# Splitting ten weight blocks of a hybrid encoder layer in two pieces each instead of one

## The chip, the core and the metric

The kernel runs on one core of a Trainium2 chip. The metric is the device time of one execution in microseconds (us). The engines are called as the profile calls them: PE (matrix multiply), PEld (its weight loads), DVE (vector), ACT (scalar and activation), POOL, and SP, which issues nearly all DMAs. Each engine works through its own list of instructions in a fixed order that was settled when the program was built; an instruction that waits holds up everything behind it on its engine.

## The reference, cut to what matters

One layer serves 512 prompt tokens and 64 sample tokens with the same weights:

```
proj = rmsnorm(x) @ w_in              # 1024 -> conv inputs, z, a, b, qd, kd, vd
oa = gated_delta_rule(conv(...)) ; oa = rmsnorm(oa) * silu(z)
ob = rmsnorm(differential_attention(qd, kd, vd))   # 4 heads of 128 columns
h = x + concat(oa, ob) @ w_out
h = h + memory_attention(rmsnorm(h)) ; h = h + square(relu(rmsnorm(h) @ W1)) @ W2
```

The gated delta rule works in chunks: for each chunk a unit triangular 128x128 system per head is inverted, and a state is carried from chunk to chunk.

## The kernel before

Weights come in blocks of 128 columns: a tile `raw` of [128, 8, 128], that is eight row blocks of 128 rows. All arithmetic is float32 made of two rounded parts, so each block is split by `split_weights` into a high part `wh` (a cast on ACT, L161) and a low part `wl = raw - wh` (a subtraction on DVE, L162). `project` then runs two column ranges of the tokens (256, then 320), and in each the eight row blocks in turn, every one with the products high x high, high x low and low x high, into one PSUM bank of the tag `pr`, of which there are three. There are three buffers for `raw` and two each for `wh` and `wl`, so the split of a block can begin when the block two before it has gone through PE.

The middle of the program holds these pieces:

- `project_z` (L635): four blocks, whose result goes through Silu. In the lists they are `pr_246` to `pr_262`.
- `gdn_prep` (L649) prepares a chunk of the delta rule: transposes, score products, then levels 2, 4, 8, 16, 32 of a blockwise inversion. A level is two transposes into the bank of a chunk's tag and `Dt,B` products, a copy X on ACT (L762), a masked copy Y on DVE (L763), products `Y,X` on PE, and two subtractions on DVE (L770, L771) with which the next level begins. Even chunks use bank `g0`, odd chunks `g1`. After the levels come a transpose of Dt, `Dt,At` products, a copy on ACT (L779), `X,Y` products and a negated copy on DVE (L783).
- `gdn_scan` (L811) carries the state: `on,X` products in bank `gs`, DVE (L830), products with the state and KQ, `vn,kd`, then a norm over ACT (L801), DVE (L802), POOL and DVE (L809), and a transpose of `on`.
- `diff_project` (L961) projects q, k and v of an attention head, one block each; `diff_head` does the attention itself.

The source has `prep` of chunk 0, then for each chunk the prep of the next one, `project_z` (once) and the scan; then the four heads. A list scheduler with estimated costs turns that into the engines' orders. It pulls the blocks of `project_z` and of the first two heads forward between the dependent steps of the delta rule, where they serve PE as filler. Instructions under `tc.high_priority()`, as the splits are, go ahead of others that are ready.

Of the kernel before, what the change touches and what calls it, by code (L numbers as in the profile page):

```python
# [8 lines left out]
F32 = mybir.dt.float32  # L9
F32R = mybir.dt.float32r  # L10
AF = mybir.ActivationFunctionType
ALU = mybir.AluOpType
# [3 lines left out]
P = 128  # L16
D = 1024
KT = 8
# [19 lines left out]
def hybrid_layer_kernel(  # L38
# [10 lines left out]
    V, A, G = nc.vector, nc.scalar, nc.gpsimd  # L49
# [29 lines left out]
    def nm(s):  # L79
        uid[0] += 1  # L80
        return f"{s}_{uid[0]}"

    def pair(slot, dt=F32):

        return up.tile([P, 2, 4, T], dt, tag=f"u{slot}", name=nm("u"))
# [6 lines left out]
    def small(tag, shape, bufs=None, dt=F32):  # L92
        tag = SHARED.get(tag, tag)
        bufs = 1 if tag in ("vn", "on", "S", "qz") or tag[:-1] in ("At", "Dt", "Y") else 2
        return sp.tile(shape, dt, tag=tag, name=nm(tag), bufs=bufs)
# [4 lines left out]
    def bank(tag="ba"):  # L100
        return ps.tile([P, 512], F32, tag=tag, name=nm(tag), bufs=BANKS[tag])
# [4 lines left out]
    def mm(out, lhsT, rhs, start=True, stop=True, pin=False, skip_group_check=False):  # L106
        i = nc.tensor.matmul(out, lhsT, rhs, start=start, stop=stop, skip_group_check=skip_group_check)  # L107
        if pin:
            tc.keep_in_program_order(i)

    def tr(out, in_, pin=False):
        n = in_.shape[0]
        i = nc.tensor.transpose(out, in_, ident[:n, :n])  # L113
        if pin:
            tc.keep_in_program_order(i)
# [36 lines left out]
        nc.sync.dma_start(raw, w[:, c0 : c0 + P].rearrange("(k p) n -> p k n", p=P))  # L152
        return raw

    def split_weights(w, shape):
        raw = wp.tile(shape, F32, tag="raw", name=nm("raw"), bufs=3)
        nc.sync.dma_start(raw, w.rearrange("(k p) n -> p k n", p=P))
        wh = wp.tile(shape, F32R, tag="wh", name=nm("wh"))
        wl = wp.tile(shape, F32R, tag="wl", name=nm("wl"))
        with tc.high_priority():  # L160
            A.copy(wh, raw)  # L161
            V.tensor_tensor(wl, raw, wh.bitcast(F32), ALU.subtract)  # L162
        return wh, wl

    def weights(w, c0, kt=KT):

        return split_weights(w[:, c0 : c0 + P], [P, kt, P])

    def project(w, x, evac, kt=KT, halves=HALVES, between=None):


        for a0, n in halves:
            b = bank("pr")
            for k in range(kt):
                low_part = lambda: mm(b[:, :n], w[1][:, k, :], x[k // 4][:, 0, k % 4, a0 : a0 + n], start=False, stop=False)
                if k == kt - 1:
                    low_part()
                high_parts(b, w[0], x, k, a0, n, kt)
                if k < kt - 1:
                    low_part()  # L180
            if between and a0 == 0:
                between()
            evac(b[:, :n], a0, n, None if a0 else b[:, 256:])

    def high_parts(b, w, x, k, a0, n, kt=KT):
        xk = x[k // 4][:, :, k % 4, a0 : a0 + n]
        if a0 == 0:
            mm(b.rearrange("p (j n) -> p j n", j=2), w[:, k, :], xk, start=k == 0, stop=k == kt - 1)
        else:
            mm(b[:, :n], w[:, k, :], xk[:, 0], start=k == 0, stop=False)  # L190
            mm(b[:, :n], w[:, k, :], xk[:, 1], start=False, stop=k == kt - 1)

    def add_to(dst, b, more):
        A.copy(dst, more)
        V.tensor_tensor(dst, b, dst, ALU.add)
# [50 lines left out]
    xs = [pair(i, F32R) for i in (0, 1)]  # L246
    w2 = w_in[0]
# [387 lines left out]
    def project_z():  # L635
        for h in range(H):
            def evac(b, a0, n, more):
                z = zs[:, h, a0 : a0 + 256]
                with tc.high_priority():
                    if more is not None:  # L640
                        add_to(z, b, more)
                        b = z
                    A.activation(z, b[:, :256], AF.Silu)
                    if a0:
                        A.activation(zsample[:, h, :], b[:, 256:], AF.Silu)

            project(weights(w2, 1536 + h * P), xs, evac)

    def gdn_prep(c, nb, L):  # L649
        (ck, kb), (cq, qb), (_, vblk) = (blocks(typ, c, L) for typ in (1, 0, 2))  # L650
# [310 lines left out]
    def diff_project(h):  # L961
        hs = slice(h * P, (h + 1) * P)
        if h < 2:
            qn = [od[:, 2 * h + j, :SEQ].bitcast(F32R) for j in range(2)]
        else:
            qn = [small(tag, [P, SEQ], dt=F32R) for tag in ("Y0", "Y1")]
        tags = ("kd", "vb", "X", "KQ") if h % 2 else ("At0", "At1", "Dt0", "Dt1")
        ks = [small(tag, [P, SEQ], dt=F32R) for tag in tags]
        stacked[h] = ks[:2], ks[2:]
        for kind, base in (("q", 2056), ("k", 2568), ("v", 3080)):  # L970
            def evac(b, a0, n, more):
                ts_ = slice(a0, a0 + n)
                t0 = slice(a0, min(a0 + n, SEQ))
                n0 = t0.stop - a0

                def parts(dst, src):
                    A.copy(dst[0][:, t0], src[:, :n0])
                    V.tensor_tensor(dst[1][:, t0], src[:, :n0], dst[0][:, t0].bitcast(F32), ALU.subtract)

                if kind == "q":  # L980
                    d = b
                    if more is not None:
                        d = qn[1][:, ts_].bitcast(F32)
                    with tc.high_priority():
                        if more is not None:
                            add_to(d, b, more)
                        parts(qn, d)
                    if a0:
                        for c in range(2):
                            R = slice(64 * c, 64 * c + 64)  # L990
                            A.copy(qz[R, R], d[R, n - DEC :])
                            for j in range(2):
                                nc.sync.dma_start(
                                    qs[h % 2][64 * j : 64 * j + 64, c, :SEQ].bitcast(F32), qn[j][R].bitcast(F32)
                                )
                    return
                d = small("zr", [P, 320])[:, :n] if kind == "v" else kdT[:, h, ts_]
                with tc.high_priority():
                    if more is not None:
                        add_to(d, b, more)  # L1000
                    else:
                        V.tensor_copy(d, b)
                if kind == "k":
                    parts(stacked[h][0], d)
                    if a0:
                        first_, second_ = ([x.bitcast(F32) for x in pair_] for pair_ in stacked[h])
                        for j in range(2):
                            for R in (slice(0, 64), slice(64, P)):
                                nc.sync.dma_start(second_[j][R], first_[j][64:])
                        for j in range(2):  # L1010
                            nc.sync.dma_start(first_[j][64:], first_[j][:64])
                bt = bank()
                for t in range(2):
                    tr(bt[:, t * P : (t + 1) * P], d[:, t * P : (t + 1) * P])
                if a0:
                    tr(bt[:DEC, 256:384], d[:, 256:])
                src, t2 = bt[:, :256].rearrange("p (t d) -> p t d", t=2), slice(a0 // P, a0 // P + 2)
                if kind == "v":
                    A.copy(vtm[:, t2, hs], src)
                    if a0:  # L1020
                        A.copy(vs[:DEC, h, :], bt[:DEC, 256:384])
                else:
                    ko = small("ko", [P, 3, P])
                    A.copy(ko[:, :2], src)
                    nc.sync.dma_start(o_dk_p[0, 0, a0 : a0 + 256, h, :].rearrange("(t p) d -> p t d", p=P), ko[:, :2])
                    if a0:
                        A.copy(ko[:DEC, 2], bt[:DEC, 256:384])
                        nc.sync.dma_start(o_dk_s[0, 0, :, h, :], ko[:DEC, 2])

            project(weights(w2, base + h * P), xs, evac)  # L1030
        nc.sync.dma_start(o_dv_p[0, 0, :, h, :].rearrange("(t p) d -> p t d", p=P), vtm[:, :, hs])
        nc.sync.dma_start(o_dv_s[0, 0, :, h, :], vs[:DEC, h, :])

# [100 lines left out]
    for h in range(H):  # L1134
        diff_project(h)
        next(sample, None)
        if h == 0:
            diff_cache()
        finish = diff_head(h, finish)
        next(sample, None)  # L1140
# [237 lines left out]
    raws, parts = {}, {}  # L1378
# [334 lines left out]
```

## Time and profile before

| | |
|---|---|
| time, median of 3 runs | 979.46 us (977.47 to 980.0) |
| the profiled execution's own time | 979.61 us |
| its span, first to last instruction | 976.5 us |
| granted PE clock, mean | 0.997 |
| PE, DVE, ACT busy | 98%, 71%, 55% |
| the splits of the ten blocks | from about 97 to 199 us of the span |

The profiled time is 3.1 us longer than its span, for what lies around the program, and 0.15 us above the median. A view of groups lists, for a line, engine and pair of tiles, the count, the busy time, the mean duration of one and the idle time of the engine just before. A timeline row gives start, duration, engine, line, operation, tiles and count, and in brackets the engine's idle time before it with what ended it. PE's matmuls overlap, so its durations exceed the distance from one start to the next.

### The profile page before, as it was taken

To read this page: it belongs to the slowest core of one execution; us is meant where nothing else is said; L and a number is where in the kernel's file an instruction comes from. 1 tells how busy PE (TensorE), PEld (TensorE's weight loads), DVE (VectorE), ACT (ScalarE), POOL (GpSimd) and SP (SyncE) were. 2 spreads that over 40 slices of the span, in tenths; PEclk is the share of its full clock that TensorE was granted. 3 is DMA by queue.
4 is the path that set the end of the run, shared out by engine and by line. 5 is a ranking of instruction groups with operands and counts; after the bars stand their busy time and mean duration, and the time that the engine had idled before them with its cause. 6 is when DMAs were issued, how large, how long until landed. Compare 5 with 4: busy or idle time off the path is not lost.

```text
span 976.5 us, 16991 instructions
## 1 busy us (share of the span) xinstructions
PE 961.3 (98%) x6399; PEld 890.0 (91%) x6399; DVE 689.2 (71%) x1507; ACT 537.4 (55%) x1218; POOL 64.9 (7%) x159
## 2 busy tenths in 40 slices
PE   9999999999999999999999999999999999999996
PEld 7999998988888878999999999999999999999996
DVE  5656777777767776666557887657767779978674
ACT  7664775444556765435445567665544445555444
POOL 3341020211010000000000000000000000000000
PEclk9999999999999999999999999999999999999998
DMA  7442342130644656341121413222222322233202
GB/s 206 114 144 77 78 141 66 33 77 22 177 132 116 225 174 204 87 130 44 44 65 44 140 56 108 87 87 87 87 87 87 87 87 87 87 88 87 65 23 97
DMA packets 124915, 96.01 MB, mean 98 GB/s; under 512 B 6204, under 2 KB 112846, under 8 KB 124322
## 3 DMA queue, kind: packets, MB, share of 16 engines
q1 hardware_dynamic: 124466, 94.28, 33.5%
q8 instruction: 50, 0.82, 0.4%
q10 hardware_dynamic: 368, 0.66, 0.2%
q14 instruction: 31, 0.25, 0.1%
HBM read 79.93 MB, written 9.75 MB: 92 GB/s over the span
## 4 chain that ended last, share of the span: by engine, by line
PE 55%; DVE 3%; issue 2%; DMA 1%; ACT 1%; POOLq 0%; POOL 0%; ACTq 0%; DVEq 0%
PE pr L107 33%; PE ba L107 11%; PE g L107 7%; PE gs L107 4%; DMA raw<-in_w_ff_dram 1%; PE ba L113 1%; DVE wl L162 1%; DVE u L1353 1%; DMA raw<-in_w_mem_o_dram 0%; DVE u L1215 0%; ACT wh L161 0%; ACT u L1592 0%; DVE u L1217 0%; DVE w2l L1353 0%; DVE f L1368 0%
## 5 line engine op out<-in xcount | busy, mean ns | idle before, releaser
L107 PE MATMUL pr<-u,wh 128*128 128x320 f32 (+2 forms) x1240 | 326.4, 341 | 0.0
L107 PE MATMUL pr<-u,wl 128*128 128x256 f32 (+1 forms) x816 | 225.8, 300 | 0.0
L107 PEld LDWEIGHTS pr<-u,wh 128*128 128x128 f32 x1240 | 211.9, 189 | 14.9 <-ACT u L288 0.4
L107 PEld LDWEIGHTS pr<-u,wl 128*128 128x128 f32 x816 | 150.4, 189 | 2.4 <-DVE wl L388 0.2
L162 DVE TENSOR_TENSOR wl<-raw,wh 128x1024 fp32r<-128x1024 f32 x65 | 79.5, 1223 | 54.9 <-ACT wh L161 54.8
L161 ACT CAST wh<-raw 128x1024 fp32r<-128x1024 f32 x65 | 68.2, 1049 | 64.6 <-PE pr L107 50.0
L107 PE MATMUL pr<-u,w2h 128*128 128x320 f32 (+1 forms) x384 | 98.5, 341 | 0.0
L1453 ACT CAST w2h<-r 128x512 fp32r<-128x512 f32 x56 | 34.7, 619 | 86.6 <-PE pr L107 84.7
L107 PE MATMUL pr<-f,w2h 128*128 128x320 f32 (+1 forms) x288 | 74.4, 341 | 0.1
L107 PEld LDWEIGHTS pr<-u,w2h 128*128 128x128 f32 x384 | 65.0, 188 | 4.4 <-ACT u L1538 0.3
L107 PE MATMUL pr<-u,w2l 128*128 128x256 f32 (+1 forms) x256 | 65.2, 296 | 0.0
L1540 DVE TENSOR_TENSOR u<-u,pr 128x256 f32<-128x256 f32 x96 | 42.4, 451 | 17.3 <-PE pr L107 16.6
L107 PE MATMUL ba<-u,wl 128*128 128x288 f32 x360 | 52.9, 296 | 0.1
L107 PEld LDWEIGHTS pr<-f,w2h 128*128 128x128 f32 x288 | 48.7, 188 | 4.1 <-issue 1.3
L208 POOL TENSOR_TENSOR tiny<-tiny,nhalf 128x1 f32<-128x1 f32 (+4 forms) x10 | 7.9, 788 | 650.6 <-DVE tiny L1606 514.3
L107 PEld LDWEIGHTS ba<-u,wl 128*128 128x128 f32 x360 | 49.2, 188 | 0.6 <-ACT keep L1490 0.5
L107 PE MATMUL pr<-f,w2l 128*128 128x256 f32 (+1 forms) x192 | 48.9, 296 | 0.0
L107 PEld LDWEIGHTS pr<-u,w2l 128*128 128x128 f32 x256 | 47.0, 189 | 1.5
L1454 DVE TENSOR_TENSOR w2l<-r,w2h 128x512 fp32r<-128x512 f32 x56 | 38.5, 688 | 9.5 <-ACT w2h L1453 9.4
L107 PE MATMUL pr<-wh,u 128*128 128x512 f32 x128 | 41.7, 400 | 0.1
L1499 ACT ACTIVATE c<-c 128x288 f32<-128x288 f32 x48 | 20.6, 443 | 28.6 <-DVE c L1498 28.6
L107 PEld LDWEIGHTS pr<-f,w2l 128*128 128x128 f32 x192 | 35.2, 189 | 1.1
(552 smaller groups left out, 2025.5 us busy)
## 6 DMA issues: line engine op xcount, KB each, us to landing
raw<-in_w_ff_dram SPq DMA_DIRECT2D x36, 512.0 KB
raw<-in_w_in_dram SPq DMA_DIRECT2D x28, 512.0 KB
r<-in_w_ff_dram SPq DMA_DIRECT2D x56, 256.0 KB
raw<-in_w_mem_k_dram SPq DMA_DIRECT2D x8, 512.0 KB
raw<-in_w_mem_v_dram SPq DMA_DIRECT2D x8, 512.0 KB
raw<-in_w_out_dram SPq DMA_DIRECT2D x8, 512.0 KB
raw<-in_w_mem_q_dram SPq DMA_DIRECT2D x8, 512.0 KB
raw<-in_w_mem_o_dram SPq DMA_DIRECT2D x8, 512.0 KB
```

The lines of the kernel that those rows point to most:

```text
L107: i = nc.tensor.matmul(out, lhsT, rhs, start=start, stop=stop, skip_group_check=skip_group_check)
L113: i = nc.tensor.transpose(out, in_, ident[:n, :n])
L161: A.copy(wh, raw)
L162: V.tensor_tensor(wl, raw, wh.bitcast(F32), ALU.subtract)
L208: G.tensor_tensor(out, in_, bc(nhalf[: in_.shape[0], 0:1], list(in_.shape)), ALU.pow)
L1353: V.tensor_tensor(lo, src, hi.bitcast(F32), ALU.subtract)
L1453: A.copy(wh, src)
L1454: V.tensor_tensor(wl, src, wh.bitcast(F32), ALU.subtract)
L1499: A.activation(c, c, AF.Relu)
L1540: V.tensor_tensor(am, am, b, ALU.add)
```

## The change

`split_weights` takes a number of parts and does the cast and the subtraction once for each part of the row blocks. With two parts a block is cast, subtracted, cast, subtracted in halves of four row blocks (128x512). The four blocks of z and the six of the first two heads are done so; all others as before. The DMA that loads `raw` stays whole.

```
     def split_weights(w, shape, parts=1):
...
         with tc.high_priority():
-            A.copy(wh, raw)
-            V.tensor_tensor(wl, raw, wh.bitcast(F32), ALU.subtract)
+            step = shape[1] // parts
+            for k in range(0, shape[1], step):
+                c = slice(k, k + step)
+                A.copy(wh[:, c], raw[:, c])
+                V.tensor_tensor(wl[:, c], raw[:, c], wh[:, c].bitcast(F32), ALU.subtract)
...
-            project(weights(w2, 1536 + h * P), xs, evac)
+            project(weights(w2, 1536 + h * P, parts=2), xs, evac)
...
-            project(weights(w2, base + h * P), xs, evac)
+            project(weights(w2, base + h * P, parts=2 if h < 2 else 1), xs, evac)
```

Lines of the changed source stand three further down (L771 becomes L774). The instructions are the same but for ten more casts and ten more subtractions, but the scheduler orders all engines anew from the first z block to the attention of the first heads; behind that PE's list is the same again. Two places are shown. The numbers behind the tiles are those of the program.

PE, where the filler of the first two heads runs out, before: `pr_539` is the last block of that kind (v of the second head), `g1_360` to `g1_363` the end of chunk 3's inversion, `g0_386` and higher the beginning of chunk 4's.

```order
L107 MATMUL g1_360_2265<-Y1_342_2184,X_341_2183 128x128 x2
L107 MATMUL g0_386_2369<-u_1_75 128x128
L107 MATMUL gs_415_2469<-S_267_1889,u_1_75 128x128 x2
L113 MATMUL g1_361_2269<-ident_79,Dt1_343_2185 128x128 x4
L107 MATMUL gs_415_2469<-S_267_1889,u_1_75 128x128
L107 MATMUL g0_388_2375<-u_4_78,u_1_75 128x128 x2
L107 MATMUL pr_539_3120<-u_7_94,wh_534_3092 128x320
L107 MATMUL g1_362_2276<-Dt1_343_2185,At1_335_2160 64x64 x4
L113 MATMUL g0_391_2381<-ident_79,u_1_75 128x128 x2
L107 MATMUL g1_363_2282<-X_341_2183,Y1_342_2184 64x64 x4
L113 MATMUL g0_397_2395<-ident_79,X_393_2389 128x128 x2
L107 MATMUL gs_417_2476<-on_416_2474,X_341_2183 128x128 x2
```

And the same place in the changed program.

```order
L107 MATMUL pr_539_3140<-u_7_94,wh_534_3110 128x320 x2
L107 MATMUL g0_386_2377<-u_1_75 128x128 x2
L107 MATMUL g1_357_2258<-Y1_342_2192,X_341_2191 128x128 x2
L107 MATMUL g0_388_2383<-u_4_78,u_1_75 128x128 x2
L113 MATMUL g1_359_2266<-ident_79,Y1_342_2192 128x128 x2
L107 MATMUL g1_359_2266<-Dt1_343_2193,B1_358_2264 128x128 x2
L113 MATMUL g0_391_2389<-ident_79,u_1_75 128x128 x2
L113 MATMUL g0_397_2403<-ident_79,X_393_2397 128x128 x2
L107 MATMUL g1_360_2273<-Y1_342_2192,X_341_2191 128x128 x2
```

The last filler of the first two heads now stands ahead of `g1_357`, a level and a half earlier in chunk 3's inversion; between it and `g1_362` there is no more `pr` product.

DVE at the same place, before: `wl_609` is the low part of the third head's k block, whose cast waits until `pr_539` has left its buffer free.

```order
L709 SCALAR_TENSOR_TENSOR At0_387_2372<-g0_386_2369,tg_381_2353,Y0_385_2365 128x128 x2
L733 SCALAR_TENSOR_TENSOR B0_396_2392<-lev_1271,At0_387_2372 128x256
L827 TENSOR_TENSOR on_416_2474<-vb_338_2171,gs_415_2469 128x512
L713 TENSOR_TENSOR KQ_389_2378<-g0_388_2375,Y0_385_2365 128x256
L734 TENSOR_TENSOR X_393_2389<-ident_79,B0_396_2392 128x256
L716 TENSOR_TENSOR vb_390_2379<-g0_391_2381,tg_382_2356 128x256
L162 TENSOR_TENSOR wl_609_3420<-raw_607_3417,wh_608_3419 128x1024
L783 TENSOR_SCALAR X_341_2183<-g1_363_2282 64x4x64
```

And in the changed program.

```order
L712 SCALAR_TENSOR_TENSOR At0_387_2380<-g0_386_2377,tg_381_2361,Y0_385_2373 128x128
L165 TENSOR_TENSOR wl_609_3440<-raw_607_3437,wh_608_3439 128x1024
L773 TENSOR_TENSOR Y1_342_2192<-Dt1_343_2193,g1_357_2258 128x8x16
L712 SCALAR_TENSOR_TENSOR At0_387_2380<-g0_386_2377,tg_381_2361,Y0_385_2373 128x128
L774 TENSOR_TENSOR Dt1_343_2193<-Dt1_343_2193,g1_357_2258 128x16x16
L736 SCALAR_TENSOR_TENSOR B0_396_2400<-lev_1271,At0_387_2380 128x256
L716 TENSOR_TENSOR KQ_389_2386<-g0_388_2383,Y0_385_2373 128x256
L737 TENSOR_TENSOR X_393_2397<-ident_79,B0_396_2400 128x256
L719 TENSOR_TENSOR vb_390_2387<-g0_391_2389,tg_382_2364 128x256
L766 SCALAR_TENSOR_TENSOR Y1_342_2192<-lev_1271,g1_359_2266 128x256
```

This undivided subtraction has moved from the end of chunk 3's inversion to a place ahead of the two subtractions that close level `g1_357`, and the masked copy for `g1_359` stands behind four operations of chunk 4.

More of the change, by code (lines that the diff above doesn't have):

```diff
@@ L153, in load, with split_weights @@
         return raw
-    def split_weights(w, shape):
+    def split_weights(w, shape, parts=1):
         raw = wp.tile(shape, F32, tag="raw", name=nm("raw"), bufs=3)
@@ L160, in split_weights, with weights @@
         with tc.high_priority():
-            A.copy(wh, raw)
-            V.tensor_tensor(wl, raw, wh.bitcast(F32), ALU.subtract)
+            step = shape[1] // parts
[3 more added lines that the diff above has]
+                V.tensor_tensor(wl[:, c], raw[:, c], wh[:, c].bitcast(F32), ALU.subtract)
         return wh, wl
-    def weights(w, c0, kt=KT):
-        return split_weights(w[:, c0 : c0 + P], [P, kt, P])
+    def weights(w, c0, kt=KT, parts=1):
+        return split_weights(w[:, c0 : c0 + P], [P, kt, P], parts)
     def project(w, x, evac, kt=KT, halves=HALVES, between=None):
```

## The prediction

> **What bounds the kernel now.** First the page: which engine is full, and how long the operations take that the change cuts up.
>
> ```profile
> span 976.5 us, 16991 instructions
> PE 961.3 (98%) x6399; PEld 890.0 (91%) x6399; DVE 689.2 (71%) x1507; ACT 537.4 (55%) x1218; POOL 64.9 (7%) x159
> ...
> L162 DVE TENSOR_TENSOR wl<-raw,wh 128x1024 fp32r<-128x1024 f32 x65 | 79.5, 1223 | 54.9 <-ACT wh L161 54.8
> L161 ACT CAST wh<-raw 128x1024 fp32r<-128x1024 f32 x65 | 68.2, 1049 | 64.6 <-PE pr L107 50.0
> L1453 ACT CAST w2h<-r 128x512 fp32r<-128x512 f32 x56 | 34.7, 619 | 86.6 <-PE pr L107 84.7
> ```
>
> PE is busy 98% of the span, so a gain can only come out of its gaps or of fewer instructions on it, and the change leaves its instructions alone. Hence PE's waits, then its gaps by stretch.
>
> ```profile
> PE gs L113 <- DVE on L809: 0.9, 2, 0.6
> PE pr L107 <- DVE wl L162: 0.7, 1, 0.7
> PE g L107 <- DVE Y L763: 0.7, 2, 0.4
> PE g L107 <- ACT Y L779: 0.6, 1, 0.6
> PE gs L107 <- DVE X L783: 0.4, 1, 0.4
> ```
>
> ```profile
> 127.00:225.00 98.00, 97.25 (x751) 90.55 (x750) 76.25 (x182) 49.86 (x113) 15.46 (x29) 1.00 0.24 62
> 225.00:247.00 22.00, 19.50 (x152) 16.95 (x151) 16.47 (x48) 10.53 (x33) 5.17 (x13) 1.00 0.15 38
> 247.00:345.00 98.00, 97.04 (x607) 84.52 (x607) 71.03 (x232) 63.74 (x207) 5.82 (x13) 1.00 0.57 164
> 345.00:360.00 15.00, 14.19 (x76) 11.09 (x75) 10.80 (x18) 10.25 (x25) 1.36 (x2) 1.00 0.43 126
> ```
>
> The columns after the stretch's length are busy PE, PEld, DVE, ACT and POOL with counts, then the granted clock. PE's gaps from 127 to 360 us are 0.75 + 2.50 + 0.96 + 0.81 = 5.0 us, half of them in the 22 us where the filler of the first two heads has run out and the inversion and scan of the delta rule stand alone. The clock is 1.00 throughout, so the gaps cost only themselves. In the whole span PE waited once for a `wl`, and that is not one of the ten blocks:
>
> ```profile
> 358.41 0.49 PE L107 MATMUL pr<-wl,u 128*128 128x512 f32 x1 [0.71 <-DVE wl L162]
> ...
> 120.45 1.23 DVE L162 TENSOR_TENSOR wl<-raw,wh 128x1024 fp32r<-128x1024 f32 x1 [1.34 <-ACT wh L161]
> ...
> 124.54 0.28 PE L107 MATMUL pr<-u,wl 128*128 128x256 f32 x1
> ```
>
> The first is a memory weight. The other two are the last z block: its `wl` is done at 121.68 and PE reaches it at 124.54, 2.9 us later.
>
> **The change part by part.** *The halves themselves.* A first half would be ready after 0.62 us of cast and about 0.69 of subtraction instead of 1.05 and 1.22, some 0.96 us earlier. That hides under the 2.9 us lead, so I cost it at 0. The added twenty instructions take little, since neighbours on an engine overlap:
>
> ```profile
> 248.28 1.29 DVE L202 TENSOR_TENSOR u<-u,u 128x512 fp32r<-128x512 f32 x2
> ...
> 355.61 1.26 ACT L201 CAST u<-u 128x576 fp32r<-128x576 f32 x2
> ```
>
> Two subtractions of 512 take 1.29 us together against 1.22 whole: +0.07. Two casts of 0.69 take 1.26, an overlap of 0.12, so two of 0.619 take 1.12 against 1.05: +0.07. Ten blocks: 10 x 0.14 = 1.4 us of engine time. It is off the path while filler covers it; DVE is busy 78% from 127 to 225 us, so some of it will fall into dependent chains. I take 0.3, with 0 and 1.4 as ends.
>
> [...]
>
> *The new order.* This is what decides. The rows of the tail before, from the last filler of the second head (`pr_539`) to the first of the third (`pr_605`):
>
> ```profile
> 233.46 0.39 PE L107 MATMUL pr<-u,wh 128*128 128x320 f32 x1
> 233.78 0.68 PE L107 MATMUL g<-Dt,At 128*64 128x64 f32 x8
> 233.88 1.05 ACT L161 CAST wh<-raw 128x1024 fp32r<-128x1024 f32 x1 [0.16 <-PE pr L107]
> 234.96 0.37 ACT L779 COPY Y<-g 64x256 f32<-64x256 f32 x1
> 235.28 1.22 DVE L162 TENSOR_TENSOR wl<-raw,wh 128x1024 fp32r<-128x1024 f32 x1
> 236.87 0.71 PE L107 MATMUL gs<-on,X 128*128 128x128 f32 x4 [0.39 <-DVE X L783]
> ...
> 240.09 0.39 PE L107 MATMUL g<-Dt,B 128*128 128x128 f32 x2
> 240.31 0.39 PE L107 MATMUL gs<-vn,KQ 128*128 128x128 f32 x2
> ...
> 245.99 0.66 PE L113 MATMUL gs<-ident,on 128*128 128x128 f32 x4
> 246.40 0.48 PE L107 MATMUL pr<-u,wh 128*128 128x512 f32 x1
> ```
>
> Call T the end of the last filler, 233.85. The chain reaches the scan's `on,X` at T+3.02 and the next filler at T+12.55.
>
> In the new order T comes with `g1_357`'s level unfinished. Steps from T, with these and the following durations:
>
> ```profile
> 228.07 0.28 DVE L770 TENSOR_TENSOR Y<-Dt,g 128x128 f32<-128x128 f32 x1
> 228.59 0.41 DVE L771 TENSOR_TENSOR Dt<-Dt,g 128x256 f32<-128x256 f32 x1
> ...
> 232.87 0.43 DVE L733 SCALAR_TENSOR_TENSOR B<-lev,At 128x256 f32<-128x256 f32 x1
> ```
>
> - The cast of the third head's k block waits for `pr_539`: T+1.1. Its subtraction follows, 1.22: T+2.3. DVE can do nothing in between, though `Y,X` of `g1_357` is through at T+0.9: what is queued behind the subtraction are L770 and L771 of that level, and PE waits for them.
> - L770, half of L709, L771, overlapping by 0.09: T+3.15. `Dt,B` of `g1_359` on PE: T+3.65.
> - The masked copy for `g1_359` stands behind four operations of chunk 4 like L733, each 0.33 after the one before: 4 x 0.33 and the copy's own 0.42 make T+4.85.
> - `Y,X`, L771, transposes of Dt: 0.45 + 0.45 + 0.5: T+6.3. Products of chunk 4 stand ahead of `Dt,At`: T+6.6.
> - From `Dt,At` to `on,X` it took 236.87 - 233.78 = 3.09, of which 0.5 was L779 waiting behind the cast (matmuls done 234.46, copy 234.96); that cast is now past. 2.6: T+9.2.
> - From `on,X` to the next filler as before, 246.40 - 236.87 = 9.53: T+18.7.
>
> So the stretch without filler grows by 18.7 - 12.55 = 6.2 us. Work on PE moves into it as well: ten products of 128 columns at 0.22 (240.09 to 240.31 for one in two passes), six transposes at 0.10 (245.99 to 246.40 for four), and 0.8 of chunk 4's later levels, in all 3.6. The rest is wait: +2.6. The lower end is +1.3, if the chain behind `on,X` loses 0.8 because fewer steps of chunk 4 share its engines, and the stretch before it another 0.5; the upper is +3.1, if L779 waits 0.5 as before.
>
> *Loads.* A `raw` buffer goes back to SP after the second half, 0.1 us or so later than before, and the next block's load keeps its place ahead of the attention's copies on SP's queue. DMA engines are busy 24% and 15% of the first two stretches (last column but one), so I cost this at 0.
>
> *Elsewhere.* The two waits for `on` at L809 (0.9) sit where filler stood thin; the new order has `pr` products or transposes in front of each of the three such transposes. I credit half: -0.5. Against that, the second head's sample scan has less filler behind it:
>
> ```profile
> 286.78 0.68 PE L107 MATMUL gs<-u,aT 128*128 128x128 f32 x4 [0.46 <-DVE on L809]
> ```
>
> Ahead of this stood seven 320-column and seven 256- or 512-column products, now ten of the latter kind: 0.5 less cover, +0.5. And in each of the first two heads four `pr` products between the last transposes of the attention weights and `gs<-u,aT` are gone, so the copy from PSUM shows: +0.3 each, +0.6. All of these may be 0.
>
> Sum: 2.6 + 0.3 - 0.5 + 0.5 + 0.6 = 3.5 on 979.61 (the profiled execution, 0.15 above the median): **983.1 us**.
>
> **The rivals.** *The tail grows by no more than moves into it* (no change). For it: the chain after `on,X` has less of chunk 4 beside it than before, and the waits for L809 may go altogether. +1.3 - 0.9 = +0.4: 980.0, between 976.7 and 982.5. Against it: DVE waiting for a cast that waits for PE is plain in the order.
>
> *Shorter pieces close the gaps* (faster). A cast or subtraction ahead of a step of the inversion holds it 0.4 to 0.5 us less, and the scheduler spread the filler anew. PE's gaps from 127 to 360 us are 5.0, less the 0.71 for the memory weight 4.3; with 70% gone it is 979.6 - 3.0 = 976.6. It decides if the gap from 225 to 247 us falls below 1 us. Against it: that gap lies behind the ten splits, at an undivided one. [...]
>
> *The halves do nothing.* The order shows PE's fifth row block waiting for ACT a second time, so the parts are told apart; the change does what it says.
>
> **How the numbers follow.** A measurement of this kernel tells about 0.3%, 2.9 us, from no change. The tail as worked out, 0.48: slower, its own range 982.4 to 986.0 (+3.1 in place of 2.6, all 1.4 of engine time, no credit and both later waits: 979.6 + 5.6 = 985.2, and 0.8 for the scatter of a median, where the runs before span 2.5). No change, 0.30. Faster, 0.22, down to 976.6. The range holds the first two and most of the third: 976.5 to 986.0.
>
> **What would show it.** Right: no `pr` product between chunk 3's `g1_357` and `on,X`, a gap of 1 us or more on PE in front of `g1_359`'s transposes with DVE L773 as the releaser, a wait of DVE for the cast just before, and 4.5 us or more of gaps in the 20 us before the third head's first block instead of 2.5. The waits of PE for `wl` in z and the first heads stay none. Wrong: gaps there of 2.5 us or less; or the same gaps and a shorter span, which would mean that PE lost time before that these rows do not show.

## The result, and the profile after

The changed kernel takes 984.58 us (median of 6, 983.71 to 987.29) beside 979.26 us for the kernel before on the same chip: 1.0066 times the time before, 95% interval 1.0056 to 1.0076. That is slower, by 5.3 us where 3.5 were forecast. The profiled execution of the changed kernel took 983.71 us, 4.1 more than that of before; its span is 5.2 longer. Lines of the changed source stand three further down.

The first lines of the page:

```profile
span 981.7 us, 17010 instructions
PE 961.7 (98%) x6399; PEld 890.0 (91%) x6399; DVE 690.0 (70%) x1517; ACT 538.6 (55%) x1228; POOL 64.6 (7%) x159
```

The halves in the view of groups by form:

```profile
L165 DVE TENSOR_TENSOR wl<-raw,wh 128x512 fp32r<-128x512 f32 x20 | 13.1, 685 | 7.4 <-ACT wh L164 7.4
...
L164 ACT CAST wh<-raw 128x512 fp32r<-128x512 f32 x20 | 11.8, 619 | 5.5 <-PE pr L107 5.5
```

PE has the same work and 5 us more of gaps. The halves take 0.69 and 0.62 us, as forecast; DVE and ACT are busy 0.8 and 1.2 us more. PE's waits, and its gaps by stretch (the first columns are length and busy PE, the last but two the granted clock):

```profile
PE ba L113 <- DMA p<-in_cache_diff_k_dram: 2.0, 1, 2.0
PE g L107 <- DVE At L712: 1.6, 1, 1.6
...
PE gs L107 <- ACT aT L1109: 0.8, 3, 0.3
PE pr L107 <- DVE wl L165: 0.7, 1, 0.7
PE gs L107 <- DVE on L812: 0.7, 1, 0.7
```

```profile
127.00:225.00 98.00, 97.30 (x751) 90.77 (x748) 76.89 (x186) 50.50 (x118) 17.71 (x33) 1.00 0.23 58
225.00:250.00 25.00, 20.64 (x153) 17.16 (x154) 17.41 (x52) 10.82 (x35) 3.55 (x9) 1.00 0.24 61
229.80:249.80 20.00, 15.90 (x117) 12.76 (x117) 13.06 (x39) 8.65 (x28) 1.92 (x5) 1.00 0.30 74
250.00:345.00 95.00, 91.11 (x577) 79.95 (x577) 64.14 (x211) 59.02 (x196) 5.82 (x13) 1.00 0.52 151
```

Two large waits are new: 1.6 us in the tail, where the prediction had one, and 2.0 us behind the tail for a load of cached keys, which it did not have. The two waits of transposes (L113) for `on` at L809 are gone; the one for `on` that is left (L812 here) is that of a head's sample scan. The tail, from the last filler of the second head to the first of the third:

```profile
228.93 0.46 PE L107 MATMUL pr<-u,wh 128*128 128x320 f32 x2
229.48 1.04 ACT L164 CAST wh<-raw 128x1024 fp32r<-128x1024 f32 x1
230.66 1.22 DVE L165 TENSOR_TENSOR wl<-raw,wh 128x1024 fp32r<-128x1024 f32 x1
231.80 0.28 DVE L773 TENSOR_TENSOR Y<-Dt,g 128x128 f32<-128x128 f32 x1
232.00 0.35 DVE L712 SCALAR_TENSOR_TENSOR At<-g,tg,Y 128x128 f32<-128x128 f32 x1
232.26 0.41 DVE L774 TENSOR_TENSOR Dt<-Dt,g 128x256 f32<-128x256 f32 x1
232.40 0.71 PE L107 MATMUL g<-u,u 128*128 128x128 f32 x4 [1.59 <-DVE At L712]
233.16 0.61 PE L107 MATMUL g<-Dt,B 128*128 128x128 f32 x4
...
234.98 0.71 PE L107 MATMUL g<-Y,X 128*128 128x128 f32 x4
236.28 0.60 PE L113 MATMUL g<-ident,Dt 128*128 128x128 f32 x4
237.55 0.68 PE L107 MATMUL g<-Dt,At 128*64 128x64 f32 x8
240.01 0.71 PE L107 MATMUL gs<-on,X 128*128 128x128 f32 x4 [0.16 <-DVE X L786]
...
249.83 0.50 PE L107 MATMUL pr<-u,wh 128*128 128x512 f32 x1
```

With T at 229.39, `on,X` comes at T+10.6 and the next filler at T+20.4, in place of 12.55 before. Behind it SP's queue (start, time of the issue) and the PE products that bear on it:

```profile
244.29 1.11 SPq L1012 DMA_DIRECT2D Dt<-At  x2
...
250.63 0.38 PE L113 MATMUL g<-ident,Dt 128*128 128x128 f32 x2
251.04 1.11 SPq L1012 DMA_DIRECT2D Dt<-At  x2
252.25 0.55 SPq L1039 DMA_DIRECT2D u<-in_cache_diff_v_dram  x1
252.88 0.45 SPq L1041 DMA_DIRECT2D p<-in_cache_diff_k_dram  x1
...
259.03 1.07 PE L113 MATMUL ba<-ident,p 128*128 128x128 f32 x8 [1.97 <-DMA p<-in_cache_diff_k_dram]
```

And in the kernel before:

```profile
247.47 0.53 SPq L1038 DMA_DIRECT2D p<-in_cache_diff_k_dram  x1
248.08 0.38 SPq L1036 DMA_DIRECT2D u<-in_cache_diff_v_dram  x1
...
252.13 3.19 SPq L1009 DMA_DIRECT2D Dt<-At  x4
```

Before, the load went out at 247.47, ahead of the cached values. Now it stands behind the copies `Dt<-At` of the first head's keys, and behind the 512 KB of values. The tiles of these copies are also those of the delta rule: the last two go out at 251.04, just when PE has done chunk 4's transposes of Dt (250.63 + 0.38). In the kernel before the same copies went out later still, from 252.13, but the cached keys stood ahead of them.

**Where the time went.** Orders differ, so the kernels are compared at equal work. The work of a PE instruction is the median distance from its start to the next one for its kind (shape) in the kernel before, 929.7 us in all; what a kernel has lost at some point is the time that has passed less the work done. Before and after have lost (us): 12.8 and 12.1 at 200 us of work, 19.6 and 22.1 at 230 (the end of the tail), 20.8 and 25.6 at 240, 27.1 and 32.7 at 300, 38.8 and 43.9 at the end. So the tail gave +3.3, the keys +2.2, the two heads' attention +0.9, the rest -0.5; the -0.7 ahead of the tail is mostly the start, where profiled executions scatter by 0.9 before any split.

### The profile page after: what moved, and what is told of

Its sections match the earlier page's. It is cut to its first block, busy times and chain, and to the rows that moved or that the text cites. A ratio compares the mean times of both kernels' runs of the same rounds, so it can differ in the third digit from the quotient of the medians.

```text
span 981.7 us, 17010 instructions
## 1 busy us (share of the span) xinstructions
PE 961.7 (98%) x6399; PEld 890.0 (91%) x6399; DVE 690.0 (70%) x1517; ACT 538.6 (55%) x1228; POOL 64.6 (7%) x159
## 4 chain that ended last, share of the span: by engine, by line
PE 60%; issue 2%; ACT 1%; POOLq 0%; POOL 0%; DVE 0%; ACTq 0%
PE pr L107 38%; PE ba L107 11%; PE g L107 7%; PE gs L107 4%; PE ba L113 1%; ACT u L1595 0%; ACT c L1503 0%; POOLq L1712 0%; POOL tiny L211 0%; ACT w L1355 0%; ACT wh L1355 0%; DVE u L1218 0%; ACT c L1499 0%; ACT u L1507 0%; ACTq L1600 0%
## 5 line engine op out<-in xcount | busy, mean ns | idle before, releaser
L165 DVE TENSOR_TENSOR wl<-raw,wh 128x1024 fp32r<-128x1024 f32 (+1 forms) x75 | 80.4, 1080 | 53.7 <-ACT wh L164 53.5
L164 ACT CAST wh<-raw 128x1024 fp32r<-128x1024 f32 (+1 forms) x75 | 69.5, 935 | 63.0 <-PE pr L107 48.5
```

What stands on the lines that cost most here:

```text
L164: A.copy(wh[:, c], raw[:, c])
L165: V.tensor_tensor(wl[:, c], raw[:, c], wh[:, c].bitcast(F32), ALU.subtract)
```

## The experiments

The forecasts of the first four speak of 984.6 for the changed kernel and 979.3 for the one before; the chips of the experiments gave 978.1 to 978.7 for the latter, so ratios are compared. The letters A to G name theories; the forecast in which one first stands says what it holds. All runs at a glance: ratio to before with its interval; levels of chunk 3's inversion (`g<-Dt,B` of four) left when chunk 2's scan starts `on,X` (one that begins up to 0.5 us ahead counts as left); and what was lost, in us, up to 230 us of work, from 230 to 240 and from 240 to 300.

```
kernel                      ratio (95%)              levels  to 230  to 240  to 300
before                      1                             4    19.6     1.3     6.2
changed                     1.0066 (1.0056 to 1.0076)     5    22.1     3.5     7.1
e1  keys ahead of values    1.0056 (1.0043 to 1.0069)     5    22.6     1.3     8.1
e2  wl held behind vb       1.0032 (1.0019 to 1.0044)     5    22.8*    1.6     5.6
e3  z only                  0.9979 (0.9970 to 0.9988)     3    16.2     2.1     6.4
e4  heads only              1.0005 (0.9996 to 1.0014)     4    17.7     1.6     8.3
e5  e1 + v held             1.0045 (1.0032 to 1.0058)     5    21.4     1.3     8.1
e6  k, v held               1.0032 (1.0020 to 1.0045)     5    22.0     1.7     5.9
e7  before + k, v held      1.0009 (1.0000 to 1.0018)     4    20.5*    1.6     6.0
e8  before + keys late      1.0006 (0.9997 to 1.0015)     4    19.3     1.6     6.6
e9  half of q held          1.0047 (1.0035 to 1.0059)     5    26.1*    1.0     6.3
e10 q held                  1.0011 (1.0003 to 1.0020)     4    19.8     1.1     6.4
e11 before + q held         1.0024 (1.0016 to 1.0033)     3    18.5     3.0     6.2
e12 second head undivided   1.0000 (0.9991 to 1.0009)     4    19.8     1.1     7.2
* with stretches at half clock (last section)
```

**The two new waits.** In `diff_cache`:

```
-        nc.sync.dma_start(cvv, ...)
         for bi in range(2):
             nc.sync.dma_start(ckr[bi], ...)
+        nc.sync.dma_start(cvv, ...)
+        for bi in range(2):
             b = bank()
```

> The changed kernel with one edit: the two loads of the cached keys stand ahead of the load of the cached values in the code, so that on SP's queue the 256 KB of keys go out one place before the 512 KB of values, not behind them. The subtraction wl of the third head's k block stays where the change put it on DVE. Theory A (the 5.3 us are two waits that the new order makes, the cached keys' landing at 2.0 us and the stall behind the undivided subtraction at 1.6 us, and small ones): the wait of ba on the DMA of p (2.0 us) is gone or under 0.3, the wait of g on DVE At stays at 1.6, and the time is 984.6 - 2.0 = 982.6 (982.0 to 983.2). Theory B (the 20 further instructions and the shorter pieces cost the time wherever they stand): 984.6, unchanged within 0.5. Theory C (the tail is simply longer, its fillers ran out, and the DMA's wait only fills a hole that another wait would fill): 984.6 to 984.0, with a new PE wait of over 1 us within the 20 us after it.

The wait went: the transposes of the keys came at 255.84 without one, and 2.2 us less were lost at that place. The ratio fell by 0.0010 only, inside both intervals. The profiled execution lost 1.0 us more than the changed kernel from 240 to 300 us of work, and 1.3 more from 775 to 850, where the orders are alike. Theory A's price for this wait is shown at its place, not in the sum: on the forecast's scale e1 takes 1.0056 x 979.3 = 984.8, which is what theory B had. Theory C's new wait of over 1 us did not come either; from 250 to 285 us PE waits for nothing over 0.15 us.

The next holds cast and subtraction of the third head's k block behind the last DVE product of chunk 4's preparation:

```
         V.tensor_tensor(vb, bv, nk..., ALU.mult)
+        turned.update(vb=nc.cur_bb.bb.instructions[-1])
...
+            if h == 2 and kind == "k":
+                with tc.issue_after(turned["vb"]):
+                    w = weights(w2, base + h * P)
```

> The changed kernel with one edit: cast and subtraction of the third head's k block are held behind the last product of the last chunk's preparation (vb of chunk 4) on DVE, which is where the kernel before has that subtraction. Halves of z and of the first two heads stay. The order of SP's loads follows: the cached keys go out ahead of the cached values again. Theory A: both waits are gone (g on DVE At from 1.6 to under 0.4, ba on the DMA of p from 2.0 to under 0.3), and the time is 984.6 - 3.6 = 981.0 (980.2 to 982.0); what is then left over the kernel before, 1.7 us, is what the further small waits and the instructions cost. Theory B: 984.6 within 0.5. Theory C: one of the waits comes back in another place, 983 to 984.6.

The time came out near theory A's (981.25 beside 978.19; on the forecast's scale 1.0032 x 979.3 = 982.4, where A said up to 982.0), but not for its reason. The wait for `At` fell to 0.6 only, and one of 1.0 came in another place, as C had it.

```profile
PE g L107 <- DVE Y L767: 1.2, 2, 1.0
PE gs L107 <- DVE vn L834: 0.8, 1, 0.8
...
PE g L107 <- DVE At L712: 0.6, 1, 0.6
```

```profile
233.30 1.21 DVE L165 TENSOR_TENSOR wl<-raw,wh 128x1024 fp32r<-128x1024 f32 x1
234.44 0.41 DVE L767 SCALAR_TENSOR_TENSOR Y<-lev,g 128x256 f32<-128x256 f32 x1
...
234.90 0.81 PE L107 MATMUL g<-Y,X 128*128 128x128 f32 x4 [1.02 <-DVE Y L767]
```

The subtraction now holds the masked copy of the next level, and `Y,X` comes at 234.90 as it did at 234.98 in the changed kernel. The `Dt,B` products ahead of it had come at 231.96 in place of 233.16, 0.3 of it from an earlier start; so the subtraction did cost about 1 us at its old place, and it costs 1.0 us at the new one. Up to this point e2 has lost as much as the changed kernel (16.5 and 16.7 us); in the 3.4 us behind it PE ran at half clock (last section), so its 22.8 at the end of the tail is not the order's alone. The gain lies behind the tail, in the keys' load that went out earlier and in the attention. Moving that subtraction within the tail did not shorten the tail; a tail without it was not run.

**Parts alone.** `parts=2` only in `project_z`, and only in `diff_project` for the first two heads:

> Only the four z blocks in halves (8 of the 20 further instructions); the blocks of all four heads are undivided. The order of SP's loads is that of the kernel before but for one place, and the third head's subtraction falls later than before on DVE, into a level of the last inversion. Theory A: no wait for the cached keys, at most a wait of about 1 us where the subtraction stands between two steps of the inversion; 979.3 to 980.5. Theory B (cost by instruction, 5.3 us over 20): 979.3 + 2.1 = 981.4. Theory C (what the halves do is to reshuffle the fillers, by chance for better or worse): anything from 977 to 984, without relation to the two waits.

> Only the six blocks of the first two heads in halves (12 of the 20 further instructions); z is undivided. On SP the cached keys go out ahead of the cached values; the third head's subtraction stands behind the last state's sum, where fillers are near. Theory A: neither of the two waits, 979.3 to 980.5. Theory B: 979.3 + 3.2 = 982.5. Theory C: anything from 977 to 984, without relation to the two waits.

Eight of the twenty further instructions made the kernel faster by 0.21%, twelve left it as it was, and all twenty cost 0.66%. Theory B, a price for each instruction, falls; so does A's forecast for e3, which came out 2 to 3 us better; A's for e4 held. In e3 PE is nearly full where the tail was:

```profile
205.00:250.00 45.00, 44.37 (x339) 39.82 (x337) 31.86 (x84) 21.35 (x61) 5.74 (x14) 1.00 0.31 84
```

The kernel before has 42.50 busy there, the changed one 40.63:

```profile
205.00:250.00 45.00, 42.50 (x326) 38.12 (x325) 31.84 (x84) 20.20 (x57) 5.47 (x14) 1.00 0.18 47
```

```profile
205.00:250.00 45.00, 40.63 (x312) 35.67 (x312) 32.02 (x86) 17.75 (x51) 7.47 (x18) 1.00 0.19 48
```

What differs is how far the chain has come when the tail begins. The start of chunk 1's scan products in before, changed and e3, one row each:

```profile
182.58 1.06 PE L107 MATMUL gs<-on,X 128*128 128x128 f32 x8
```

```profile
188.96 1.06 PE L107 MATMUL gs<-on,X 128*128 128x128 f32 x8
```

```profile
180.44 1.06 PE L107 MATMUL gs<-on,X 128*128 128x128 f32 x8
```

From 127 to 190 us PE is busy 62.5 or 62.6 of 63 us in all three, so the 6.4 us by which the changed kernel's chain is later are work that the new order put ahead of it. Most of it is filler (119.1 against 113.5 us by the count in e12's forecast below), which is missing in the tail.

**Filler held back.** `project` gets an instruction behind which PE holds the products of one block (`hold`). In e5 to e7 it is the `Y,X` of the first level of chunk 3's inversion, and held are the second head's v block (e5) or that and the second half of k; in e9 to e11 it is the transposes that open chunk 2's inversion, and held are the second half of the second head's q block (e9) or all of it:

```
-        for a0, n in halves:
+        for a0, n in halves:
+            with tc.issue_after(hold[0]) if hold and a0 in hold[1] else nullcontext():
```

> The changed kernel with the cached keys loaded first (as in e1_keys_first) and one more edit: the products of the second head's v block are held on PE until the first level of the fourth chunk's inversion has its products. The halves stay. Theory D (new, from the first four runs): what the tail costs is the length of the inversion and scan that is left when the filler is used up. At the first copy of that inversion (g1_347) the filler still to come is 5.8 us of products in the kernel before, 3.1 in the changed one and in e1 and e2, 8.8 in e3, 8.0 in e4; the time that PE lost in the tail beside its work was 5.0, 8.1, 8.1, 8.9, 2.2 and 2.4: the two add up to 11 within 0.6 but for e2 (12.0). With the edit 5.8 are left, so D expects 5.2 lost in the tail and 984.2 - 2.9 = 981.3 (980.3 to 982.3). Rival E (what is held back leaves steps of the chunk before bare, and the loss only moves ahead): 984.2 within 0.7, with 2 us or more lost before the tail.

> The changed kernel with the second half of the second head's k block and the whole of its v block held on PE until the first level of the fourth chunk's inversion has its products. The halves stay; by the order the cached keys go out ahead of the cached values. 9.0 us of filler are left at g1_347. Theory D: 11 - 9.0 = 2.0 lost in the tail, 6.1 less than in e1: 978.1 (977 to 979.5), at or below the kernel before although all ten blocks are in halves. Rival E: 984.2 within 0.7.

> The kernel before, without halves, with the same products held on PE as in e6_kv_held. 9.0 us of filler are left at g1_347 in place of 5.8. Theory D: 1.8 to 2.2 lost in the tail in place of 5.0, 979.0 - 3.0 = 976.0 (975 to 977). Rival E: 979.0 within 0.7.

D falls in e6 and e7: what was spared in the tail had been lost ahead of it. (For e5, 1.0045 x 979.0 = 983.4 lies between D's range and E's.) E6 lost 6.4 us from 180 to 200 us of work, where the changed kernel lost 1.1, and stood at 22.0 by the end of the tail. E holds for the loss up to the tail's end within about 1 us in all three, though not for the time of e6: 2.9 us came from behind the tail, where the keys' wait was gone. The next run asks what a late load costs by itself; the first keys of the kernel before are held behind the values:

```
         nc.sync.dma_start(cvv, ...)
+        late = nc.cur_bb.bb.instructions[-1]
...
+            with tc.issue_after(late):   # bi == 0
                 nc.sync.dma_start(ckr[bi], ...)
```

> The kernel before with one edit: the load of the first half of the cached keys is held behind the load of the cached values on SP's queue, as it came out in the changed kernel; no halves. By its landing (2.0 us of wait in the changed kernel) 979.0 + 1.5 to 2.0 = 980.5 to 981.0, if that wait costs its length; if the time is given back later, as e1 suggests (its wait of 2.0 went and the median fell by 1.0), 979.5 to 980.0.

```profile
248.50 0.44 SPq L1040 DMA_DIRECT2D p<-in_cache_diff_k_dram  x1
...
252.73 1.06 PE L113 MATMUL ba<-ident,p 128*128 128x128 f32 x8 [0.31 <-DMA p<-in_cache_diff_k_dram]
```

The order of the two loads costs 0.3 us there and nothing that the ratio shows. The 2.0 us need the whole queue to be late as well: the changed kernel issues this load at 252.88, 4.4 us later. Nor does the late queue alone cost them: in e1 the load went out at 252.76, ahead of the values, and PE did not wait.

Holding earlier, where PE loses nothing yet, was to bring the chain forward:

> The changed kernel, halves kept, with the second half of the second head's q block held on PE behind the first transposes of the third chunk's inversion (g0_294, at about 186 us, where PE loses nothing yet). Theory F (corrected by e5 to e7): what PE loses up to 249 us is set by the filler already spent when the third chunk's inversion starts. Spent there, and lost up to the end of the tail: 117.0 and 19.6 in the kernel before, 118.9 and 22.1 in the changed one (22.6, 22.8, 21.4, 22.0 in e1, e2, e5, e6, which share its 118.9), 117.0 and 20.5 in e7, 114.1 and 16.2 in e3, 113.9 and 17.7 in e4. Holding filler later than that (e5 to e7) moved the loss ahead and left the sum. Here 116.5 are spent: F expects 19.1 to 20.1 lost up to the tail's end. The cached keys go out ahead of the cached values, so what follows is as in the kernel before, 19.2: 978 to 980, ratio 0.999 to 1.002. Rival E (held filler only moves the loss ahead, wherever it is held): 22 lost up to the tail's end as in e6, 981 to 982, ratio 1.003 to 1.004.

> As e9_q2_held with the whole q block of the second head held; 113.9 of filler are spent at g0_294, as in e4 (and 114.1 in e3). Theory F: 16 to 18 lost up to the tail's end, 975.5 to 977.5, ratio 0.997 to 0.999: faster than the kernel before with all ten blocks in halves. Rival E: 981 to 982; if the steps ahead of g0_294 cannot use the time, the loss stands between 180 and 200 us.

> The kernel before, no halves, with the whole q block of the second head held as in e10_q_held; 113.9 of filler spent at g0_294 in place of 117.0. Theory F: 16.5 lost up to the tail's end in place of 19.6, ratio 0.996 to 0.998, 975 to 976.5. Rival E: 978 to 979, ratio 1.000, as in e7.

F falls as well: by their medians all three are slower than it says, e9 by 2.5 us, e10 by 1.5 and e11 by 3.7. E falls too, in e10, which is 2 us faster than it says, and in e11, which is 1.2 slower. PE waited at the hold itself (for `X` 2.4 us in e9, 1.8 in e10, 3.1 in e11). In e11, 1.9 us more went to a wait for a `Dt<-At` copy behind the tail, at 258.34. But e10 has all ten blocks in halves and a ratio of 1.0011: with another order on PE the same split costs a sixth of what it cost. Its chain is no earlier at chunk 1's scan (188.44), and 16.2 us are lost by 180 us of work, where the changed kernel had lost 11.0; from there to 230 it loses only 3.6, where the changed kernel lost 11.1, and four levels are left in place of five. It also has the cached keys ahead of the values, so the 0.55% between the two is not the tail's alone. The last run takes the halves from the second head (`h < 1`) and was forecast from the order of its filler (the `on,X` that it speaks of is the one at 182.58 above, of chunk 1's scan):

> The changed kernel with the blocks of the second head undivided again (z and the first head in halves, 14 of the 20 further instructions). Theory G (after e9 to e11, where filler that is held back only moved the loss): the loss follows from how much filler the order puts ahead of the chain between 127 and 190 us, while PE is full. Filler spent when the third scan's first product on,X comes, and lost up to the end of the tail: 113.5 and 19.6 in the kernel before, 119.1 and 22.1 in the changed one, 112.2 and 16.2 in e3, 112.1 and 17.7 in e4. Here it is 114.9: 19.6 to 21.0 lost up to the tail's end, the scan's on,X at 183 to 186 us (182.6 before, 189.0 in the changed kernel). The cached keys go out ahead of the cached values, so what follows is as in the kernel before: 978 to 980.5, ratio 0.999 to 1.002. Rival B (by count of instructions): 978.1 + 14/20 x 5.3 = 981.8, ratio 1.004.

```profile
183.72 1.06 PE L107 MATMUL gs<-on,X 128*128 128x128 f32 x8
```

That came: 183.7, 19.8 lost, ratio 1.0000 where counting instructions gave 1.004. Read afterwards, the table goes roughly by levels: three left, 16.2 and 18.5 lost up to 230 us of work; four, 17.7 to 20.5; five, 21.4 and more. That is an order seen in these runs, not one that was forecast and then tested. Nor is it the whole time: e4 and e11 lost 1.9 and 1.1 us less than the kernel before by the end of the tail, and neither is faster.

## Why the prediction was right, point by point

- *Halves at 0, instructions at 0.3.* The first is right: PE waits for no `wl` of the ten blocks (its one wait for a `wl`, 0.72 us at 364.06, is for a memory weight). The second was not measured by itself; e10, which has all twenty instructions, is 0.11% or 1.1 us above the kernel before, inside the ends of 0 and 1.4.
- *Tail, +2.6 (1.3 to 3.1).* It measured +3.3, a little above the upper end; the stretch without filler grew by 7.9 us (20.4 - 12.55) where 6.2 were forecast. The steps held within 0.2 up to L774: cast done at T+1.1, subtraction at T+2.5 (forecast 2.3), L774 at T+3.3 (3.15). `Dt,B` was through at T+4.4 (3.65), because products of chunk 4 stood ahead of it on PE and had been released only at 232.40. The masked copy came 0.7 late, because the fourth of chunk 4's operations waited 0.27 for PE and they stood apart, and `Dt,At` 1.6 late, since more of chunk 4's products lay before it. The gap stands one instruction ahead of where it was put: `g<-u,u` waits for the second half of L712, which is queued behind the subtraction, and not `g1_359`'s transposes for L773. The 20 us before the third head's first block have 4.1 us of gaps, where 4.5 were asked for and 2.5 or less would have spoken against it.
- *"What is queued behind the subtraction are L770 and L771 of that level, and PE waits for them".* The order is as read, but the first to wait on PE is a product of chunk 4, and as the cause of the longer tail it is not shown: e2 took the subtraction to the next level, and the tail stayed. The runs point to the step before it, "T comes with `g1_357`'s level unfinished": with one level fewer left (e10, e12) less is lost.
- *Loads at 0.* This is the step that failed. It followed one queue entry, the next block's `raw`, and bounded the rest by the DMA engines' load. What counted was the order on SP: the keys' load fell behind copies of the first head's keys, which wait for chunk 4's inversion to be done with their tiles, and behind the values. 2.0 us of wait, 2.2 lost in the profile, about 1 in e1's ratio.
- *Elsewhere: -0.5, +0.5, +0.6.* The waits for `on` went whole (-0.9), the sample scan's grew by 0.2 only (0.46 to 0.7), the aT copies show 0.8.
- *The rivals.* "No more than moves into it" missed a level's price. "Shorter pieces close the gaps" happened, in e3: halves of z alone close the tail, but by the order and not by the pieces. Before the change PE waited for no `wl` of the ten blocks (its one wait for a `wl`, 0.71 us at 358.41, is for a memory weight), and e3's only such wait is of the same 0.7 us; so an earlier first half had nothing to give.
- *The range.* The forecast lay 1.8 us short of the measured 5.3, and the keys' 2.2 us are what it left out. The range of 976.5 to 986.0 also held no change and most of a gain, so that the time fell inside it says little; what speaks for the working is the tail.
- *The clock* was taken as 1.00 throughout. In the profiled execution it is, up to 975 us; three of the six executions show a mean of 0.995 and took 984.9 to 987.3, the others 0.996 to 0.997 and 983.7 to 984.3. The faster three have a median of 983.84, 4.6 us above the kernel before; the other 0.7 us of the median go with the lower clock.

Not settled: why the scheduler puts more filler ahead of the chain with all ten blocks divided, and less with four or six; and which part of the order, the filler ahead of the chain or the levels left at its end, sets the loss in the tail.

## What to carry to other kernels

Where a list scheduler sets the order, price an edit by the order that comes out, on every engine that issues: first how far the dependent chain has come when the independent work runs out, then each queue's entries that stand behind a new wait. A wait found at a named instruction is not yet its cause; move that instruction and see whether the stretch gets shorter. Work held back by hand pays only if the chain can use the time at that point; here the loss mostly moved ahead, and the fastest kernel measured was simply the part of the change whose order was good (z alone, 976.5 us).

## What was not expected of the hardware

In three profiled executions PE's granted clock was 0.50 for a while in the middle of the kernel, each time behind a stretch in which PE was about half busy. It stayed so for 3.40 us in e2 and 3.38 in e7, and for 6.81 in e9. (In e9 it was so a second time, from 189.65 for 3.37 us, behind 3.41 us that were busy 30%.) From e2, e7 and e9, a stretch of 3.41 us ahead, about as long as the one at 0.50 in e2 and e7, and the stretch itself:

```profile
231.98:235.39 3.41, 1.80 (x14) 1.28 (x13) 2.80 (x6) 0.94 (x3) 0.00 (x0) 1.00 0.00 0
235.40:238.80 3.40, 3.21 (x18) 2.66 (x18) 1.22 (x4) 1.30 (x4) 0.31 (x1) 0.50 0.62 159
```

```profile
205.44:208.85 3.41, 1.65 (x13) 1.49 (x14) 3.21 (x7) 0.82 (x2) 0.00 (x0) 1.00 0.00 0
208.86:212.24 3.38, 3.06 (x15) 2.66 (x13) 1.38 (x4) 1.27 (x3) 0.30 (x1) 0.50 0.00 0
```

```profile
237.42:240.83 3.41, 1.89 (x20) 1.44 (x19) 1.84 (x3) 1.83 (x5) 0.00 (x0) 1.00 0.16 32
240.84:244.24 3.40, 2.62 (x11) 2.32 (x11) 1.37 (x4) 0.50 (x3) 0.00 (x0) 0.50 0.44 127
244.25:247.65 3.40, 3.40 (x16) 3.40 (x17) 0.30 (x2) 0.71 (x3) 0.00 (x0) 0.50 0.01 2
```

PE was busy 53%, 48% and 55% of the stretch ahead. But such a share alone does not bring the clock down: in the changed kernel's profile two such stretches (52% and 43% busy) passed at 1.00, and in e11's one that was emptier still (10%):

```profile
229.60:233.01 3.41, 1.77 (x13) 1.58 (x14) 3.40 (x9) 1.24 (x2) 0.00 (x0) 1.00 0.02 2
255.60:259.01 3.41, 1.46 (x10) 1.21 (x10) 0.82 (x3) 0.00 (x0) 0.00 (x0) 1.00 0.92 263
```

```profile
183.80:187.21 3.41, 0.33 (x3) 0.10 (x3) 3.41 (x6) 1.52 (x3) 0.00 (x0) 1.00 0.00 0
```

What tells these from the others is not shown. PE's longest single wait in e2's stretch was 1.02 us; in e11's it was 3.08, and the clock stayed. Between 45 and 900 us the emptiest 3.41 us of the kernel before (from 233.60) are busy 70%, and in the runs beside e1 to e11 its mean clock is 0.997 or 0.998 in every execution. What such a stretch costs was not measured by itself.
